# A diffusion block on one core: the second MLP matrix gets a VectorE and ScalarE order written by hand

## The chip, the cores and the metric

The kernel runs on one core of a Trainium2 chip. The metric is the device time of one execution in microseconds (us); the median of three runs before the change is 1617.91 us. A core has a matrix engine (TensorE, "PE" in the profile; its weight loads are "PEld"), an engine for elementwise work on two operands (VectorE, "DVE"), one for functions and casts of one operand (ScalarE, "ACT"), GpSimd ("POOL") and SyncE ("SP"). Here the last two only issue transfers (DMAs) between the device's main memory and the on-chip memory; each has a queue of its own. TensorE accumulates in PSUM, which has eight banks per partition.

## The reference

One layer over 512 tokens of width 2048. The second half of the layer is the MLP, whose second matrix is where the change lies:

```python
def sqrelu_mlp(h, w1, w2):
    return jnp.square(jax.nn.relu(h @ w1)) @ w2
...
x = x + g1 * rms_norm(y_lat, norm_g[i, 1])
x = x + g2 * rms_norm(sqrelu_mlp(modulate(rms_norm(x, norm_g[i, 2]), sh2, sc2), w_mlp_in[i], w_mlp_out[i]), norm_g[i, 3])
```

The hidden width is 8192, so `w2` is 8192 x 2048 in 32-bit floats. Ahead of the MLP come the adaLN vectors, a Fourier mixer and its output matrix.

## The kernel before

**Arithmetic.** Every 32-bit product is made of three faster ones. `split` (L117 to L120) casts an operand on ScalarE to a rounded `hi` and subtracts on VectorE to get the rest, `lo`. `mm3` (L122 to L125) then issues hi x lo, lo x hi and hi x hi into one PSUM bank. TensorE's first matmul of a piece of weights reads its `lo`. There are three `hi` and three `lo` buffers for weights (`NB["hi"]`, L32), in pool `sp`.

**First MLP matrix.** The hidden columns are worked in units of 256. Units 6 to 30 use a form with seven block products in place of eight (Winograd's variant of Strassen's algorithm): `unit(u)` (L779) makes A11, S1, S3, S2, A12, A22, S4, some of them from sums of weight blocks. Unit 31, the last, is done plainly by `unit_plain` (L827). The squared ReLU of each unit goes to device memory `gd` on GpSimd's queue (L647).

**Second MLP matrix.** Rows 0 to 7167 of `w2` are cut into seven chunks (`c`) of 1024 and the output columns into two halves (`j`). For each of the 14 pairs the same seven products are made, 98 in all, each with four pieces of left operand, two halves of weights of 128 x 1024, and 24 matmuls of 512 columns into two banks. The left operands of a chunk are made once by `left_in(c, s)` (L882): A11, A12 and A22 are a cast (L902) and a `lo` (L903) of a quarter of the loaded chunk; S1, S3, S2 and S4 first take a VectorE difference or sum (L891, L894, L897, L900). `g_chunk` (L876) loads a chunk. `second(c, j)` (L907) loads four weight blocks in two halves each and makes the weight sums on VectorE: for S1 (L941), S3 (L946), S2 (L950) and A22 (L954). After the splits of a product, the copies of the product before from PSUM (L928) are issued by `settle`, and one DMA on GpSimd's queue adds the tile to device memory (L930; L932 for the first chunk). `THEN` hangs further work on a product: the next chunk's load, its left operands, and in the last chunk `early`, the load and split of two units for the last part.

The rest of `w2` (hidden rows 7168 to 8191) is done plainly behind that, and the seven partial sums are gathered.

**What sets the order.** The program is traced once. A planner then orders the instructions of each engine and each transfer queue by priority (earlier traced first, `high_priority` moves a part ahead) and by when its own timeline holds them to be ready; the hardware's queues keep that order. Inside `tc.manual_schedule(engines=...)` the named engines keep the traced order among the block's instructions; the kernel uses it once before, at L582, and instructions from outside the block may stand between. `tc.issue_after(x)` queues the work of a block behind `x`. A tile of a pool waits until the slot's last reader is done. The pools of the second matrix (`ga`, `sb`, `s1`, `g4`, L860) lie in the memory of the first part's pool, so a chunk's first loads wait for the products that read there: the first two `ga` tiles lie where the left operands of S2 and S4 were.

The call sequence around the change:

```python
    with tc.high_priority(offset=AHEAD):
        g_chunk(0)
        for s in PRODUCTS:
            cast = left_in(0, s)
...
    for c in range(CHUNKS):
        for j in range(2):
            second(c, j)
    settle()
```

Of the kernel before, what the change touches and what calls it, by code (L numbers as in the profile page):

```python
# [12 lines left out]
ALU = mybir.AluOpType  # L13

P = 128
# [43 lines left out]
def block_kernel(ctx: ExitStack, tc, xs, c_l, w_mod, b_col, g_col,  # L59
# [21 lines left out]
    def hi4(shape):  # L81
        return sp.tile(shape, F32R, tag="hi4", bufs=NB["hi"], name=nm("hi"))
# [22 lines left out]
    def bank(shape=(P, 512)):  # L105
        return psp.tile(list(shape), F32, tag="ps", bufs=8 - NB["mv"], name=nm("ps"))
# [529 lines left out]
    def stream(src):  # L636
        flip[0] ^= 1
        t = raw("raw" if flip[0] else "rawm")
        nc.sync.dma_start(out=t, in_=src)
        return t  # L640
# [138 lines left out]
    def unit(u):  # L779

        b11, b12, b22, b21 = (stream(w_in_s[u - UNIT0, b].rearrange("p k f -> p (k f)")) for b in range(4))

        x_, y_ = bank(), bank()
        a_, b_, c_, d_ = x_[:, T0], x_[:, T1], y_[:, T0], y_[:, T1]

        def product(s, src, ps, start):
            wh, wl = hi4([P, 1024]), lo4([P, 1024])
            split(wh, wl, src)
            for k in range(8):
                ks = slice(k * P, (k + 1) * P)  # L790
                lh, ll = left_of(s, k)
                nc.tensor.matmul(ps, lhsT=wh[:, ks], rhs=ll, start=start and k == 0, stop=False, skip_group_check=True)  # L792
                nc.tensor.matmul(ps, lhsT=wl[:, ks], rhs=lh, start=False, stop=False, skip_group_check=True)  # L793
                nc.tensor.matmul(ps, lhsT=wh[:, ks], rhs=lh, start=False, stop=k == 7, skip_group_check=True)  # L794

        product("A11", b11, a_, True)
        flip[0] ^= 1
        both = raw("raw" if flip[0] else "rawm")
        nc.vector.tensor_add(out=both, in0=b11, in1=b12)
        product("S1", both, d_, True)  # L800
        settle()
        sn, r = tmp4([P, 4, 256]), tmp4([P, 1024])
        nc.scalar.copy(out=sn[:, 0], in_=a_)
        nc.vector.tensor_add(out=b12, in0=b12, in1=b22)
        product("S3", b12, c_, False)
        nc.scalar.copy(out=sn[:, 2:4].rearrange("p a t -> p (a t)"), in_=y_)
        nc.vector.tensor_add(out=b11, in0=b12, in1=b11)
        product("S2", b11, b_, False)
        product("A12", b21, a_, False)
        nc.vector.tensor_add(out=b12, in0=b11, in1=b21)  # L810
        product("A22", b12, c_, False)
        nc.vector.tensor_sub(out=sn[:, 1], in0=sn[:, 0], in1=b_)
        nc.vector.tensor_add(out=sn[:, 2], in0=sn[:, 2], in1=sn[:, 3])
        nc.vector.tensor_add(out=r[:, 768:1024], in0=sn[:, 1], in1=sn[:, 2])
        product("S4", b22, d_, False)
        nc.scalar.activation(out=r[:, 0:256], in_=a_, func=AF.Relu)
        nc.scalar.activation(out=r[:, 768:1024], in_=r[:, 768:1024], func=AF.Relu, scale=-1.0)

        def rest():
            nc.vector.tensor_add(out=r[:, 256:768].rearrange("p (a t) -> p a t", a=2), in0=y_.rearrange("p (a t) -> p a t", a=2),  # L820
                                 in1=sn[:, 1].unsqueeze(1).to_broadcast([P, 2, 256]))
            nc.scalar.activation(out=r[:, 256:512], in_=r[:, 256:512], func=AF.Relu)
            nc.scalar.activation(out=r[:, 512:768], in_=r[:, 512:768], func=AF.Relu, scale=-1.0)
            square_out(u, r.rearrange("p (f t) -> p f t", f=2))
        owed.append(rest)
# [44 lines left out]
    PRODUCTS = ("A11", "S1", "S3", "S2", "A12", "A22", "S4")  # L870
    pacc = {(s, j): dp.tile([P, 2, 512], F32, name=f"p{s}{j}") for s in PRODUCTS for j in range(2)}
    left = [{} for _ in range(CHUNKS)]
    first_cast = []
    raws = [{} for _ in range(CHUNKS + 1)]

    def g_chunk(c):  # L876
        gf = [buf("ga", [P, 4, 512]) for _ in range(2)]
        for j in range(2):
            nc.sync.dma_start(out=gf[j].rearrange("p u t -> p (u t)"), in_=gd[c][:, j].rearrange("p u t -> p (u t)"))
        raws[c]["g"] = gf  # L880

    def left_in(c, s):  # L882

        st = raws[c]
        gf = st["g"]
        a11, a21, a12, a22 = gf[0][:, :, T0], gf[0][:, :, T1], gf[1][:, :, T0], gf[1][:, :, T1]
        if s in ("A11", "A12", "A22"):
            src = {"A11": a11, "A12": a12, "A22": a22}[s]
        elif s == "S1":
            src = st["v"] = tmp4([P, 4, 256])  # L890
            nc.vector.tensor_sub(out=src, in0=a22, in1=a21)  # L891
        elif s == "S3":
            src = tmp4([P, 4, 256])
            nc.vector.tensor_sub(out=src, in0=a11, in1=a21)  # L894
        elif s == "S2":
            src = st["v"]
            nc.vector.tensor_add(out=src, in0=src, in1=a11)  # L897
        else:
            src = st["v"]
            nc.vector.tensor_sub(out=src, in0=src, in1=a12)  # L900
        t = buf("ga" if s == "A11" else "s1" if s == "S1" and c % 2 == 0 else "sb", [P, 2, 4, 256], F32R)
        cast = nc.scalar.copy(out=t[:, 0], in_=src)  # L902
        nc.vector.tensor_tensor(out=t[:, 1], in0=src, in1=as32(t[:, 0]), op=ALU.subtract)  # L903
        left[c][s] = t
        return cast

    def second(c, j):  # L907

        def load(b):
            return [stream(w_out_s[c, j, b, h].rearrange("p k n -> p (k n)")) for h in range(2)]  # L910

        def product(s, src):
            ps = [bank(), bank()]
            for h in range(2):
                wh, wl = hi4([P, 1024]), lo4([P, 1024])
                split(wh, wl, src[h])
                for k in range(2):
                    ks = slice(k * 512, (k + 1) * 512)
                    for i in range(2):
                        ts = slice(i * P, (i + 1) * P)  # L920
                        t = left[c][s]
                        mm3(ps[i], t[:, 0, 2 * h + k, ts], t[:, 1, 2 * h + k, ts], wh[:, ks], wl[:, ks], h + k == 0, h + k == 2)
            settle()

            def out():
                ev = g4([P, 2, 512])
                for i in range(2):
                    nc.scalar.copy(out=ev[:, i, :], in_=ps[i])  # L928
                if c:
                    nc.gpsimd.dma_start(out=pacc[s, j], in_=ev, accum_op=ALU.add)  # L930
                else:
                    nc.gpsimd.dma_start(out=pacc[s, j], in_=ev)  # L932
            owed.append(out)
            for f in THEN.get((c, j, s), ()):
                f()

        b11, b12 = load(0), load(1)
        product("A11", b11)
        both = [g4([P, 1024]) for _ in range(2)]
        for h in range(2):  # L940
            nc.vector.tensor_add(out=both[h], in0=b11[h], in1=b12[h])  # L941
        b22 = load(2)
        with tc.issue_after(first_cast[0]) if c + j == 0 else nullcontext():
            product("S1", both)
        for h in range(2):
            nc.vector.tensor_add(out=b12[h], in0=b12[h], in1=b22[h])  # L946
        product("S3", b12)
        b21 = load(3)
        for h in range(2):
            nc.vector.tensor_add(out=b11[h], in0=b12[h], in1=b11[h])  # L950
        product("S2", b11)
        product("A12", b21)
        for h in range(2):
            nc.vector.tensor_add(out=b12[h], in0=b11[h], in1=b21[h])  # L954
        product("A22", b12)
        product("S4", b22)

    oacc = []

# [19 lines left out]
            nc.vector.scalar_tensor_tensor(out=oacc[2 + i][:, right_c], in0=u2[:, h], scalar=-1.0, in1=p["S1"][:, h], op0=ALU.mult, op1=ALU.subtract)  # L979


    NEXT = {(0, "A12"): ("A11",), (0, "S4"): ("S1",), (1, "A11"): ("S3",), (1, "A12"): ("S2",), (1, "S4"): ("A12", "A22")}
    THEN = {}
    for c in range(CHUNKS - 1):
        THEN[c, 0, "S3"] = [lambda c=c: g_chunk(c + 1)]
        for (j, s), what in NEXT.items():
            THEN[c, j, s] = [lambda c=c, n=n: left_in(c + 1, n) for n in what]
        THEN[c + 1, 0, "S1"] = [lambda c=c: left_in(c + 1, "S4")]

    gts = {}  # L990

# [10 lines left out]
            g_in(u, lambda: (t[:, 0], t[:, 1]))  # L1002
        oacc.extend(buf("sb" if i else "ga", [P, D]) for i in range(4))

    THEN[CHUNKS - 1, 0, "A12"] = [early]
    with tc.high_priority(offset=AHEAD):
        g_chunk(0)
        for s in PRODUCTS:
            cast = left_in(0, s)
            if s == "S1":  # L1010
                first_cast.append(cast.ins)
            if s == "S3":
                with tc.issue_after(cast.ins):
                    act_relu2(UNITS - 1, last)
    for c in range(CHUNKS):
        for j in range(2):
            second(c, j)
    settle()

    f0, f1 = LAST[0]  # L1020
    for n in (0, 2, 1, 3):
# [150 lines left out]
```

## Time and profile before

| | us |
|---|---|
| median of 3 runs (lowest, highest) | 1617.91 (1617.63, 1619.02) |
| the profiled execution | 1621.48 |
| its span, first to last instruction | 1619.7 |
| mean granted TensorE clock in it | 0.991 |
| TensorE busy | 1566.8 |
| VectorE busy | 1251.4 |
| ScalarE busy | 853.6 |
| second matrix in it, from the first matmul of A11 on | from about 965 to 1500 |

The profile shows one execution. An engine's timeline has the start, the duration, the engine, the line, the operation, what it writes and reads, the shapes, and in brackets how long the engine idled before it and whose work ended that idle time; rows of the same kind in a row are merged, with a count (x2). TensorE's durations are modelled, so a step from one start to the next says more than a duration. A line of a helper (L119, L120, L123 to L125) stands for every caller.

### The profile page before, as it was taken

How to read it: one execution, taken by the hardware profiler on the slowest of the kernel's cores; microseconds unless marked ns; L12 is line 12 of the kernel's file. 1: busy time of each engine (PE TensorE's matmuls, PEld its weight loads, DVE VectorE, ACT ScalarE, POOL GpSimd, SP SyncE). 2: the span in 40 equal slices, each digit the busy share in tenths (PEclk: the TensorE clock that was granted, in tenths of full speed). 3: DMA queues.
4: the chain of work that ended last, by engine and by line, in shares of the span. 5: the costliest groups of instructions: out<-in, count | busy, mean ns of one | idle time of the engine just before them, and what ended most of it. 6: DMA issues, size and time to landing. Idle time of an engine off the chain costs nothing.

```text
span 1619.7 us, 24743 instructions
## 1 busy us (share of the span) xinstructions
PE 1566.8 (97%) x9753; PEld 1329.1 (82%) x9753; DVE 1251.4 (77%) x1545; ACT 853.6 (53%) x1235; POOL 106.2 (7%) x144
## 2 busy tenths in 40 slices
PE   5999998999999999999999989999999999999997
PEld 4766664678899999999999977878878787878886
DVE  7776868675888888888777659979797969767687
ACT  7443336335554545455555537757575757665442
POOL 0000000000000000000000000111111111111100
PEclk9999998999999999999999999999999999999999
DMA  9987889886255555555443456779898988888972
GB/s 380 335 294 291 327 321 358 313 310 250 98 179 187 171 172 177 188 179 185 138 130 135 143 183 245 248 199 252 199 249 215 238 219 198 203 212 199 313 280 104
DMA packets 98325, 365.09 MB, mean 225 GB/s; under 512 B 11109, under 2 KB 11125, under 8 KB 95393
## 3 DMA queue, kind: packets, MB, share of 16 engines
q1 hardware_dynamic: 78992, 294.30, 50.7%
q0 software_dynamic: 19216, 69.22, 19.8%
q8 instruction: 76, 1.25, 0.3%
q14 instruction: 41, 0.33, 0.1%
HBM read 286.92 MB, written 76.55 MB: 224 GB/s over the span
## 4 chain that ended last, share of the span: by engine, by line
PE 79%; DVE 10%; DMA 6%; issue 3%; ACT 2%; DVEq 0%; SPq 0%; ACTq 0%
PE ps L123 16%; PE ps L124 16%; PE ps L125 16%; PE ps L793 9%; PE ps L794 8%; PE ps L792 8%; PE mv L206 3%; DMA raw<-in_w_mod 3%; DVE lo L120 2%; PE mv L172 1%; DVE sb L903 1%; DVE raw L946 1%; DMA ga<-gd 1%; DMA raw<-gd 1%; ACT hi L119 1%
## 5 line engine op out<-in xcount | busy, mean ns | idle before, releaser
L120 DVE TENSOR_TENSOR lo<-raw,hi 128x1024 fp32r<-128x1024 f32 x379 | 461.0, 1222 | 185.8 <-ACT hi L119 183.6
L119 ACT CAST hi<-raw 128x1024 fp32r<-128x1024 f32 x379 | 398.3, 1051 | 316.3 <-PE ps L125 147.1
L123 PE MATMUL ps<-lo,sb 128*128 128x512 f32 x608 | 238.0, 391 | 5.7 <-DVE lo L120 5.6
L124 PE MATMUL ps<-hi,sb 128*128 128x512 f32 x608 | 236.6, 389 | 0.0
L125 PE MATMUL ps<-hi,sb 128*128 128x512 f32 x608 | 236.6, 389 | 0.0
L793 PE MATMUL ps<-big,lo 128*128 128x256 f32 x600 | 170.2, 284 | 0.0
L794 PE MATMUL ps<-big,hi 128*128 128x256 f32 x600 | 169.8, 283 | 0.0
L792 PE MATMUL ps<-big,hi 128*128 128x256 f32 x600 | 169.6, 283 | 0.0
L928 ACT COPY g<-ps 128x512 f32<-128x512 f32 x196 | 114.6, 588 | 91.9 <-PE ps L125 83.8
L123 PEld LDWEIGHTS ps<-lo,sb 128*128 128x128 f32 x608 | 114.1, 188 | 34.0 <-DVE lo L120 10.8
L125 PEld LDWEIGHTS ps<-hi,sb 128*128 128x128 f32 x608 | 114.1, 188 | 23.9
L124 PEld LDWEIGHTS ps<-hi,sb 128*128 128x128 f32 x608 | 114.1, 188 | 23.4
L793 PEld LDWEIGHTS ps<-big,lo 128*128 128x128 f32 x600 | 115.2, 192 | 0.3 <-DVE lo L120 0.2
L794 PEld LDWEIGHTS ps<-big,hi 128*128 128x128 f32 x600 | 115.2, 192 | 0.0
L792 PEld LDWEIGHTS ps<-big,hi 128*128 128x128 f32 x600 | 115.1, 192 | 0.0
L793 PE MATMUL ps<-g,lo 128*128 128x256 f32 x400 | 113.8, 285 | 1.1 <-DVE lo L120 1.0
L792 PE MATMUL ps<-s,hi 128*128 128x256 f32 x400 | 113.2, 283 | 0.0
L794 PE MATMUL ps<-s,hi 128*128 128x256 f32 x400 | 113.2, 283 | 0.0
L793 PE MATMUL ps<-s,lo 128*128 128x256 f32 x400 | 113.2, 283 | 0.0
L794 PE MATMUL ps<-g,hi 128*128 128x256 f32 x400 | 113.0, 283 | 0.0
L792 PE MATMUL ps<-g,hi 128*128 128x256 f32 x400 | 112.3, 283 | 0.0
L221 DVE SCALAR_TENSOR_TENSOR row<-raw,sil,row 128x512 f32<-128x512 f32 x105 | 78.2, 749 | 21.8 <-DMA raw<-in_w_mod 20.8
(291 smaller groups left out, 3279.6 us busy)
## 6 DMA issues: line engine op xcount, KB each, us to landing
raw<-in_w_mod SPq DMA_DIRECT2D x192, 512.0 KB, 5.4
raw<-in_w_out_s SPq DMA_DIRECT2D x112, 512.0 KB, 5.7
raw<-in_w_in_s SPq DMA_DIRECT2D x100, 512.0 KB, 3.9
pS<-g POOLq DMA_DIRECT2D x56, 512.0 KB, 6.3
pA<-g POOLq DMA_DIRECT2D x42, 512.0 KB, 7.0
raw<-in_wf SPq DMA_DIRECT2D x32, 512.0 KB, 5.5
gd<-tmp POOLq DMA_DIRECT2D x32, 512.0 KB, 3.8
ga<-gd SPq DMA_DIRECT2D x14, 1024.0 KB, 6.6
```

The costliest lines, as they stand in the source:

```text
L119: nc.scalar.copy(out=hi, in_=src)
L120: return nc.vector.tensor_tensor(out=lo, in0=src, in1=as32(hi), op=ALU.subtract)
L123: nc.tensor.matmul(ps, lhsT=ah, rhs=bl, start=start, stop=False)
L124: nc.tensor.matmul(ps, lhsT=al, rhs=bh, start=False, stop=False)
L125: nc.tensor.matmul(ps, lhsT=ah, rhs=bh, start=False, stop=stop)
L172: nc.tensor.matmul(mv[:, 256 + cb:257 + cb], lhsT=rows[:, cb * P:(cb + 1) * P], rhs=ones[:, 0:1], start=True, stop=True)
L206: nc.tensor.matmul(st["ps"][32 * j:32 * j + 32, 0:256], lhsT=cst[:, kq * 4 + j, :], rhs=t[:, j * 256:(j + 1) * 256], start=(kq == 0), stop ...
L221: nc.vector.scalar_tensor_tensor(out=rows, in0=t[:, j * 512:(j + 1) * 512], scalar=sil[:, kt:kt + 1], in1=rows, op0=ALU.mult, op1=ALU.add)
L792: nc.tensor.matmul(ps, lhsT=wh[:, ks], rhs=ll, start=start and k == 0, stop=False, skip_group_check=True)
L793: nc.tensor.matmul(ps, lhsT=wl[:, ks], rhs=lh, start=False, stop=False, skip_group_check=True)
L794: nc.tensor.matmul(ps, lhsT=wh[:, ks], rhs=lh, start=False, stop=k == 7, skip_group_check=True)
L928: nc.scalar.copy(out=ev[:, i, :], in_=ps[i])
```

## The change

The body of `second` is taken apart into `load`, `fetch`, `product` and `leave_second`, numbered through all 98 products. All VectorE and ScalarE instructions of the second matrix (but for the first two left operands) stand in a `manual_schedule` block, in the order: the two splits of product n, the copies from PSUM of product n - 2, what `THEN` hangs on n, and then `fetch(n)`, the loads and weight sums of product n + 2. The left operands of chunk 0 after the first two move from a high-priority part into `THEN`, as does the ReLU of the last unit. The chunk-0 load goes to GpSimd's queue. In unit 30 the product S4 is made before A12.

```diff
@@ in unit(u)
         product("S2", b11, b_, False)
+        if u == UNITS - 2:
+            product("S4", b22, d_, False)
         product("A12", b21, a_, False)
...
-        product("S4", b22, d_, False)
+        if u < UNITS - 2:
+            product("S4", b22, d_, False)
@@ in g_chunk(c)
-            nc.sync.dma_start(out=gf[j].rearrange("p u t -> p (u t)"), in_=gd[c][:, j].rearrange("p u t -> p (u t)"))
+            queue = nc.sync if c else nc.gpsimd
+            queue.dma_start(out=gf[j].rearrange("p u t -> p (u t)"), in_=gd[c][:, j].rearrange("p u t -> p (u t)"))
@@ in place of second(c, j)
+    SECOND = [(c, j, s) for c in range(CHUNKS) for j in range(2) for s in PRODUCTS]
...
+    def load(c, j, *of):
+        for b in of:
+            blocks[c, j, b] = [stream(w_out_s[c, j, b, h].rearrange("p k n -> p (k n)")) for h in range(2)]
+
+    def fetch(n):
+
+        if n + 2 >= len(SECOND):
+            return
+        c, j, s = SECOND[n + 2]
+        b = [blocks.get((c, j, i)) for i in range(4)]
+        add = nc.vector.tensor_add
+        if s == "A11":
+            load(c, j, 0, 1)
+        elif s == "S1":
+            load(c, j, 2)
+            both = sums[c, j] = [g4([P, 1024]) for _ in range(2)]
+            for h in range(2):
+                add(out=both[h], in0=b[0][h], in1=b[1][h])
+        elif s == "S3":
+            for h in range(2):
+                add(out=b[1][h], in0=b[1][h], in1=b[2][h])
+        elif s == "S2":
+            load(c, j, 3)
+            for h in range(2):
+                add(out=b[0][h], in0=b[1][h], in1=b[0][h])
+        elif s == "A22":
+            for h in range(2):
+                add(out=b[1][h], in0=b[0][h], in1=b[3][h])
+
+    def leave_second(n):
+        c, j, s = SECOND[n]
+        ev = g4([P, 2, 512])
+        for i in range(2):
+            nc.scalar.copy(out=ev[:, i, :], in_=held[n][i])
+        if c:
+            nc.gpsimd.dma_start(out=pacc[s, j], in_=ev, accum_op=ALU.add)
+        else:
+            nc.gpsimd.dma_start(out=pacc[s, j], in_=ev)
+
+    def product(n):
+
+        c, j, s = SECOND[n]
+        src = sums[c, j] if s == "S1" else blocks[c, j, {"A11": 0, "S3": 1, "S2": 0, "A12": 3, "A22": 1, "S4": 2}[s]]
+        ps = held[n] = [bank(), bank()]
+        t = left[c][s]
+        for h in range(2):
+            wh, wl = hi4([P, 1024]), lo4([P, 1024])
+            split(wh, wl, src[h])
...
+        if n > 1:
+            leave_second(n - 2)
+        for f in THEN.get((c, j, s), ()):
+            f()
+        fetch(n)
@@ what hangs on which product
-    NEXT = {(0, "A12"): ("A11",), (0, "S4"): ("S1",), (1, "A11"): ("S3",), (1, "A12"): ("S2",), (1, "S4"): ("A12", "A22")}
+    REST = {(1, "S2"): ("S3",), (1, "A22"): ("S2",), (1, "S4"): ("A12", "A22")}
+    NEXT = ({(0, "S4"): ("A11",), (1, "A11"): ("S1",), **REST}, {(0, "A12"): ("A11",), (0, "S4"): ("S1",), **REST})
...
+    for s, what in (("S1", ("S3",)), ("S3", ("S2",)), ("S2", ("A12", "A22")), ("A12", ("S4",))):
+        for w in what:
+            then(0, 0, s, lambda w=w: left_in(0, w))
     for c in range(CHUNKS - 1):
-        THEN[c, 0, "S3"] = [lambda c=c: g_chunk(c + 1)]
...
+        then(c, 0, "S3" if c else "A22", lambda c=c: g_chunk(c + 1))
+        for (j, s), what in NEXT[min(c, 1)].items():
+            for w in what:
+                then(c, j, s, lambda c=c, w=w: left_in(c + 1, w))
+        then(c + 1, 0, "S1", lambda c=c: left_in(c + 1, "S4"))
...
-    THEN[CHUNKS - 1, 0, "A12"] = [early]
+    then(CHUNKS - 1, 0, "A12", early)
+    then(0, 0, "A11", lambda: act_relu2(UNITS - 1, last))
     with tc.high_priority(offset=AHEAD):
         g_chunk(0)
-        for s in PRODUCTS:
...
+        for s in ("A11", "S1"):
+            left_in(0, s)
+    fetch(-2)
+    with tc.manual_schedule(engines={mybir.EngineType.DVE, mybir.EngineType.Activation}):
+        fetch(-1)
+        for n in range(len(SECOND)):
+            product(n)
+        for n in (2, 1):
+            leave_second(len(SECOND) - n)
```

## Rows read from the trace of the kernel before

**Rows 1.** The page: busy us of each engine, share of span, instructions.
```profile
PE 1566.8 (97%) x9753; PEld 1329.1 (82%) x9753; DVE 1251.4 (77%) x1545; ACT 853.6 (53%) x1235; POOL 106.2 (7%) x144
```

**Rows 2.** Waits of PE, 900 to 1540 us: total us, times, longest.
```profile
PE ps L123 <- DVE lo L120: 11.2, 9, 3.0
PE ps L124 <- DVE ga L903: 4.5, 1, 4.5
```

**Rows 3.** Timeline of PE at three places; start us, us, engine, line.
```profile
969.78 0.80 PE L124 MATMUL ps<-hi,ga 128*128 128x512 f32 x1 [4.46 <-DVE ga L903]
...
1133.36 0.39 PE L125 MATMUL ps<-hi,ga 128*128 128x512 f32 x1
1134.84 0.50 PE L123 MATMUL ps<-lo,s 128*128 128x512 f32 x1 [1.09 <-DVE lo L120]
1135.17 0.40 PE L124 MATMUL ps<-hi,s 128*128 128x512 f32 x1
...
1445.61 0.50 PE L123 MATMUL ps<-lo,ga 128*128 128x512 f32 x1 [3.05 <-DVE lo L120]
```

**Rows 4.** Windows: busy us of each engine (instructions), PE clock, DMA share, GB/s.
```profile
960.00:1000.00 40.00, 33.26 (x139) 26.49 (x138) 39.45 (x35) 26.84 (x33) 2.84 (x5) 0.96 0.43 148
...
1440.00:1480.00 40.00, 36.61 (x155) 29.42 (x154) 27.30 (x24) 22.98 (x29) 5.93 (x7) 0.96 0.86 209
```

**Rows 5.** Timeline of DVE at the start of chunk 2.
```profile
1126.75 1.22 DVE L120 TENSOR_TENSOR lo<-raw,hi 128x1024 fp32r<-128x1024 f32 x1
1127.89 2.35 DVE L941 TENSOR_TENSOR g<-raw,raw 128x1024 f32<-128x1024 f32 x2
1130.16 1.22 DVE L946 TENSOR_TENSOR raw<-raw,raw 128x1024 f32<-128x1024 f32 x1
1131.30 1.22 DVE L903 TENSOR_TENSOR sb<-tmp,sb 128x1024 fp32r<-128x1024 f32 x1
1132.43 1.22 DVE L946 TENSOR_TENSOR raw<-raw,raw 128x1024 f32<-128x1024 f32 x1
1133.57 1.22 DVE L120 TENSOR_TENSOR lo<-g,hi 128x1024 fp32r<-128x1024 f32 x1
```

**Rows 6.** Timeline of DVE at three other places.
```profile
256.04 2.74 DVE L599 SCALAR_TENSOR_TENSOR x<-big,ry,x 128x512 f32<-128x512 f32 x4
258.69 0.69 DVE L559 TENSOR_TENSOR big<-big,big 128x512 f32<-128x512 f32 x1
...
961.69 2.35 DVE L941 TENSOR_TENSOR g<-raw,raw 128x1024 f32<-128x1024 f32 x2
...
968.50 1.22 DVE L903 TENSOR_TENSOR ga<-ga,ga 128x1024 fp32r<-128x1024 f32 x1
...
1023.42 1.22 DVE L891 TENSOR_TENSOR tmp<-ga,ga 128x1024 f32<-128x1024 f32 x1 [0.53 <-DMA ga<-gd]
```

**Rows 7.** Timeline of ACT at several places.
```profile
1024.67 1.05 ACT L902 CAST s<-tmp 128x1024 fp32r<-128x1024 f32 x1 [0.32 <-DVE tmp L891]
...
1038.80 1.10 ACT L928 COPY g<-ps 128x512 f32<-128x512 f32 x2
...
1129.78 1.06 ACT L119 CAST hi<-g 128x1024 fp32r<-128x1024 f32 x1
...
1149.02 1.05 ACT L119 CAST hi<-raw 128x1024 fp32r<-128x1024 f32 x1 [1.19 <-PE ps L125]
...
1154.45 1.05 ACT L119 CAST hi<-raw 128x1024 fp32r<-128x1024 f32 x1 [1.19 <-PE ps L125]
...
1442.12 1.05 ACT L119 CAST ga<-raw 128x1024 fp32r<-128x1024 f32 x1 [2.27 <-DMA raw<-gd]
```

**Rows 8.** The chain that ended last, 940 to 985 us: start us, us, what.
```profile
954.34 7.31 DMA ga<-gd
```

**Rows 9.** Waits of the SP queue, 900 to 1500 us: total us, times, longest.
```profile
SPq L879 <- PE ps L125: 56.3, 6, 10.8
```

**Rows 10.** The page's DMA issues: KB each, median us to landing.
```profile
raw<-in_w_out_s SPq DMA_DIRECT2D x112, 512.0 KB, 5.7
```

More of the change, by code (lines that the diff above doesn't have):

```diff
@@ L872, in block_kernel @@
     left = [{} for _ in range(CHUNKS)]
-    first_cast = []
     raws = [{} for _ in range(CHUNKS + 1)]
@@ L901, in left_in @@
         t = buf("ga" if s == "A11" else "s1" if s == "S1" and c % 2 == 0 else "sb", [P, 2, 4, 256], F32R)
-        cast = nc.scalar.copy(out=t[:, 0], in_=src)
+        nc.scalar.copy(out=t[:, 0], in_=src)
         nc.vector.tensor_tensor(out=t[:, 1], in0=src, in1=as32(t[:, 0]), op=ALU.subtract)
         left[c][s] = t
[L905 to L913, printed above, removed]
-            for h in range(2):
[L915 to L926, printed above, removed]
-                for i in range(2):
[L928 to L956, printed above, removed]
@@ new lines, in block_kernel @@
+    SECOND = [(c, j, s) for c in range(CHUNKS) for j in range(2) for s in PRODUCTS]
+    blocks = {}
+    sums = {}
+    held = {}
+    def load(c, j, *of):
[12 more added lines that the diff above has]
+            both = sums[c, j] = [g4([P, 1024]) for _ in range(2)]
+            for h in range(2):
+                add(out=both[h], in0=b[0][h], in1=b[1][h])
[9 more added lines that the diff above has]
+                add(out=b[1][h], in0=b[0][h], in1=b[3][h])
@@ new lines, in leave_second @@
+    def leave_second(n):
[15 more added lines that the diff above has]
+            split(wh, wl, src[h])
+            for k in range(2):
+                ks = slice(k * 512, (k + 1) * 512)
+                for i in range(2):
+                    ts = slice(i * P, (i + 1) * P)
+                    mm3(ps[i], t[:, 0, 2 * h + k, ts], t[:, 1, 2 * h + k, ts], wh[:, ks], wl[:, ks], h + k == 0, h + k == 2)
+        if n > 1:
[3 more added lines that the diff above has]
+        fetch(n)
@@ L979, in gather, with then @@
             nc.vector.scalar_tensor_tensor(out=oacc[2 + i][:, right_c], in0=u2[:, h], scalar=-1.0, in1=p["S1"][:, h], op0=ALU.mult, op1=ALU.subtract)
-    NEXT = {(0, "A12"): ("A11",), (0, "S4"): ("S1",), (1, "A11"): ("S3",), (1, "A12"): ("S2",), (1, "S4"): ("A12", "A22")}
+    REST = {(1, "S2"): ("S3",), (1, "A22"): ("S2",), (1, "S4"): ("A12", "A22")}
+    NEXT = ({(0, "S4"): ("A11",), (1, "A11"): ("S1",), **REST}, {(0, "A12"): ("A11",), (0, "S4"): ("S1",), **REST})
     THEN = {}
-    for c in range(CHUNKS - 1):
-        THEN[c, 0, "S3"] = [lambda c=c: g_chunk(c + 1)]
-        for (j, s), what in NEXT.items():
-            THEN[c, j, s] = [lambda c=c, n=n: left_in(c + 1, n) for n in what]
-        THEN[c + 1, 0, "S1"] = [lambda c=c: left_in(c + 1, "S4")]
+    def then(c, j, s, f):
+        THEN.setdefault((c, j, s), []).append(f)
+    for s, what in (("S1", ("S3",)), ("S3", ("S2",)), ("S2", ("A12", "A22")), ("A12", ("S4",))):
+        for w in what:
+            then(0, 0, s, lambda w=w: left_in(0, w))
+    for c in range(CHUNKS - 1):
+        then(c, 0, "S3" if c else "A22", lambda c=c: g_chunk(c + 1))
[3 more added lines that the diff above has]
+        then(c + 1, 0, "S1", lambda c=c: left_in(c + 1, "S4"))
     gts = {}
@@ L1003, in early @@
         oacc.extend(buf("sb" if i else "ga", [P, D]) for i in range(4))
-    THEN[CHUNKS - 1, 0, "A12"] = [early]
+    then(CHUNKS - 1, 0, "A12", early)
+    then(0, 0, "A11", lambda: act_relu2(UNITS - 1, last))
     with tc.high_priority(offset=AHEAD):
         g_chunk(0)
-        for s in PRODUCTS:
[L1009 to L1018, printed above, removed]
+        for s in ("A11", "S1"):
[7 more added lines that the diff above has]
+            leave_second(len(SECOND) - n)
     f0, f1 = LAST[0]
```

## The prediction

> **What bounds the kernel now.** I read the busy shares first, then TensorE's waits in the second MLP matrix, then the timelines round those waits. The reader is to see in the busy shares that TensorE (PE) is the bound, at 97% of the span, with VectorE (DVE) at 77% and ScalarE (ACT) at 53% [rows 1]. A change of order can therefore give back only what PE idles in this stretch. The waits say how much that is: between 900 and 1540 us nine waits on the `lo` that VectorE makes, 11.2 us, and one on the left operand of A11 (L903), 4.5 us [rows 2]. A wait costs more than its gap. Where the gap is 1.09 us the matmul starts 1.48 us after the one before it, against 0.23 in the run of matmuls, and the next one 0.33 after that [rows 3]: 1.25 + 0.10, so 0.26 beyond the gap, 2.6 us for ten. The granted clock is 0.96 in the two 40 us windows with the long waits [rows 4], where matmuls go at the lower level after an idle PE: 0.04 x 40 = 1.6 us each, 3.2. Together 15.7 + 2.6 + 3.2 = 21.5 us is all that the stretch can give.
>
> Their causes differ. At each of five chunk starts (1134.84 is one) VectorE does five operations back to back between two `lo`, and the second `lo` is late [rows 5]; price 1.35 each. At the beginning (969.78) it did six weight sums, from 961.69 on, ahead of A11's left `lo` at 968.50 [rows 6]. At 1445.61 [rows 3] a cast waited 2.27 us for a transfer of the last units, ahead of the next weight cast [rows 7].
>
> **The change, what it takes away.** Within the block, VectorE and ScalarE get the traced order. That such a block keeps it is seen in the earlier one: the multiply of L559 runs exactly behind four L599 as traced, at 258.69 [rows 6]. A11's and S1's left operands are now traced before the block and their loads go through GpSimd's queue. Before, those loads land at 954.34 + 7.31 = 961.65 on the chain [rows 8], held behind weight loads in SyncE's queue; the last unit's moved S4 frees their memory two products earlier. VectorE is no longer busy with the six sums, so A11 starts on time. The early casts now come behind A12 of the last chunk, four products after that chunk's start, and their transfer is there by then. The five chunk-start bursts also go, since sums are issued a product earlier. So all 21.5 us go, with what comes next priced below. Moving S4 adds no instruction, and PE has no such wait in unit 30; nothing is charged. The later copies from PSUM free a pair of banks after two products instead of one; three pairs rotate and the copies (1.10 us for two [rows 7]) run beside matmuls: nothing. The chunk loads of c = 0 on GpSimd's queue stand before that queue's write of the last units, which is read only at the end: nothing.
>
> **What it adds.** The number of operations is the same, but the queue now waits in its order. Per product VectorE has two `lo`, then the left pieces that are hung on that product, then the two sums for the product after next. Prices: two sums are 2.27 us from start to start (1127.89, x2, to 1130.16 [rows 5]), so 1.135 for one operation. A left operand made by a difference is subtract, cast on ScalarE, `lo`. From the subtract at 1023.42 to its cast at 1024.67 is 1.25 [rows 6, 7], the cast takes 1.05 and 0.03 to the next start, the `lo` 1.135: 3.47. In the traced order nothing else stands between subtract and `lo`, so VectorE idles 1.2 us of it, time in which the planner before was free to put other work. Subtract, `lo` and two sums together are 5.74 us between two `lo` that PE needs.
>
> How much is free? A product lasts 5.43 us (casts at 1149.02 and 1154.45 [rows 7]). Only three `hi` and three `lo` buffers exist, so no `lo` can be earlier than about one half-product ahead, and the chunk-start burst shows the limit: five operations, 5.68 us, between the `lo` of 1126.75 and that of 1133.57, make PE 1.25 us late [rows 3, 5]. So about 4.4 us are free, and 5.74 makes it 1.33 late, 1.44 with the restart. The cover is gone, and `lo` is what is late next.
>
> Now count, with j the column half. In a full chunk (c = 1 to 5) these products carry too much: (0, S1): left S4 and sums, 5.74. (0, S4): left S1 and sums, 5.74. (1, S2): left S3 and sums, 5.74. (1, S4): the two left casts of A12 and A22, which stand behind two copies on ScalarE, their `lo`, and sums, about 5.4, late by 1.0. All others stay at 3.5 or less. After (1, S4) comes A11 with sums, so VectorE is still 0.2 behind at the next (0, S1), which becomes 1.55 late. Chunk 0 carries more: left S3 in (0, S1), S2 in (0, S3), A12 and A22 in (0, S2), S4 in (0, A12), S1 in (1, A11). Chunk 6 has left S4 alone.
>
> Sum: 12 bursts of 5.74 by themselves ((0, S4) five times, (1, S2) six, (0, S1) of chunk 0) x 1.44 = 17.3. (1, S4) six times x 1.11 = 6.7. (0, S1) of chunks 1 to 6 x 1.66 = 10.0. Chunk 0 otherwise: (0, S2) with the debt of (0, S3), 1.8; (1, A11) behind a loaded (0, S4), 2.5; two small ones, 0.6. In all 38.9 us in 28 waits. Idle times of this length (1.09 gap) show no slower matmuls behind them [rows 3], so no clock is charged.
>
> Net +38.9 - 21.5 = +17.4 us. The profiled execution is 1621.5 (span 1619.7 and 1.8 around it), so 1638.9 there; it is 3.6 above the median of the runs, 1617.9, so the median becomes about **1635 us**.
>
> Bounds of a burst, which no row shows in this form: if the cast were wholly covered, 4.54 us, 0.15 late, 0.25 with restart; 26 bursts 6.5, and the change gains 15 (1603). If each burst also caught 0.4 us of late transfers or copies, 10 more: 1645. I take 1.35 to 1.66, as the nearest row is a burst of almost the same length with its measured lateness.
>
> One rule of the Trainium skill speaks against the part on the chunk starts. The row shows a 1.09 us gap before the same product in five chunks, ended by `lo`, with the `hi` cast done at 1129.78 + 1.06 and VectorE busy throughout [rows 3, 5, 7]. "Perfetto Trace Analysis", section "Optimization Strategy", says that a gap that repeats can mean too little SBUF for the next tile, so that order would not cure it. This case's trace does not agree for these five: VectorE's queue, not a buffer, was late. By the rule the five gaps stay.
>
> **Rivals.** (a) The cast is covered and the bursts cost little: 1603. For it: ScalarE is 53% busy and could be early. Against it: the cast needs the subtract just before it in VectorE's own queue. This is the case on the other side; it decides from a burst of 0.83 us or less (21.5 / 26), that is one of some 5.2 us. (b) The gaps at chunk starts come from buffers, stay at 5 x 1.35 = 6.8, and the new order adds nothing: 1617.9 - 14.7 = 1603. Against it: the rows just named. (c) The two effects cancel, bursts at about 0.8: 1617. (d) The fixed order makes VectorE wait for weights: SyncE's queue stood up to 10.8 us for a buffer of the chunk load [rows 9], a weight tile lands in 5.7 [rows 10], against two products, 10.9, that the earlier sums leave. Late by 5.6 in six chunks, 34 us: 1669. Against it: the buffers of the next chunk's load are now free in the traced order before it is issued. (e) The block is not strictly kept and the change only repairs the two ends, about 14 us: 1604. Against it: the order at 258.69.
>
> **How the numbers follow.** Forecast 0.60, (a) 0.16, (b) 0.04, (c) 0.07, (d) 0.09, (e) 0.04. Faster by over 0.2% is (a), (b), (e): 0.24; within 0.2% (3.2 us, about what a measurement of this kernel can tell from no change) is (c): 0.07; slower 0.69. The likeliest case alone is 1627 to 1644. The range of 1602 to 1646 reaches down to half of the faster cases and leaves out (d).
>
> **What would show it.** Right: A11 of chunk 0 starts without the 4.46 us wait; no wait at 1445; some 28 waits on `lo`, before the S3 and the second half's A11 and A12 of each chunk and before its first A11, each with a VectorE row of L891 to L903 in front that idled for a cast. Wrong: fewer than ten waits, or waits ended by transfers. The prediction falls if VectorE shows other work between the subtract and its `lo`.

## The result and the profile after

| | before | after |
|---|---|---|
| median us (lowest, highest; runs) | 1617.77 (1614.90, 1619.02; 4) | 1635.82 (1632.28, 1636.98; 4) |
| ratio after / before, 95% interval | | 1.011 [1.009, 1.0131] |
| profiled execution, its span | 1621.48, 1619.7 | 1632.28, 1630.5 |

The change made the kernel 18 us slower; 1635 was forecast. The two profiled executions lie only 10.8 us apart, because the one of before lies above all runs of its kernel in this table and the one of after is the fastest of its own. Ahead of the second matrix, where the program hardly differs, the one of after is 4.8 us earlier (first matmul of A11 at 959.87 against 964.70). From that matmul to the last one of the execution it takes 660.4 us against 644.4: 16.0 us more, and this is the stretch to explain.

The page of the kernel after, busy us and share of the span, beside [rows 1]:

```profile
PE 1562.7 (96%) x9753; PEld 1322.6 (81%) x9753; DVE 1253.4 (77%) x1545; ACT 841.8 (52%) x1235; POOL 107.3 (7%) x146
```

The work is the same to a few us on each engine. What differs is who waits. First the waits of PE from 900 to 1560 us in the kernel after (total us, times, longest), which answer to [rows 2]:

```profile
PE ps L123 <- DVE lo L120: 30.6, 26, 2.1
```

Ten waits with 15.7 us have become 26 with 30.6, all on the weights' `lo`. PE's timeline of the kernel after shows the first matmuls of A11 (`ga` is its left operand), and then one wait of each of the three kinds with a gap over 1 us, all in the first full chunk:

```profile
959.87 0.61 PE L123 MATMUL ps<-lo,ga 128*128 128x512 f32 x2
960.41 0.50 PE L124 MATMUL ps<-hi,ga 128*128 128x512 f32 x1
...
1058.29 0.50 PE L123 MATMUL ps<-lo,sb 128*128 128x512 f32 x1 [1.34 <-DVE lo L120]
...
1086.96 0.50 PE L123 MATMUL ps<-lo,ga 128*128 128x512 f32 x1 [1.13 <-DVE lo L120]
1087.29 0.39 PE L124 MATMUL ps<-hi,ga 128*128 128x512 f32 x1
...
1110.16 0.50 PE L123 MATMUL ps<-lo,sb 128*128 128x512 f32 x1 [1.13 <-DVE lo L120]
```

The reader is to see that A11 now follows the last unit without a pause, where [rows 3] had 4.46 us, and that S3 (1058.29), the second half's A11 (1086.96) and its A12 (1110.16) wait, which they did not before. (S3 of chunk 0 is the one place that waited in both: 1.65 us before, 2.04 after.) The step after a gap of 1.13 is again 0.33. The windows of the kernel after, in the columns of [rows 4], stand at the full clock:

```profile
960.00:1000.00 40.00, 36.50 (x157) 28.63 (x156) 32.57 (x29) 25.85 (x32) 3.36 (x6) 1.00 0.52 186
1440.00:1480.00 40.00, 37.91 (x166) 30.69 (x165) 32.44 (x29) 26.27 (x34) 5.94 (x7) 1.00 0.80 203
```

Why `lo` is late is in VectorE's waits of the kernel after, 955 to 1500 us, and in its timeline ahead of 1086.96. L905 and L906 are now the cast and the `lo` of a left operand, L894 a left difference, L931 and L934 weight sums:

```profile
DVE lo L120 <- ACT hi L119: 81.4, 58, 4.2
DVE sb L906 <- ACT sb L905: 29.7, 31, 1.1
DVE ga L906 <- ACT ga L905: 4.1, 6, 0.7
DVE s L906 <- ACT s L905: 3.3, 3, 1.1
```

```profile
1078.79 1.23 DVE L120 TENSOR_TENSOR lo<-raw,hi 128x1024 fp32r<-128x1024 f32 x1 [1.49 <-ACT hi L119]
1079.93 1.22 DVE L894 TENSOR_TENSOR tmp<-ga,ga 128x1024 f32<-128x1024 f32 x1
1082.27 1.23 DVE L906 TENSOR_TENSOR s<-tmp,s 128x1024 fp32r<-128x1024 f32 x1 [1.12 <-ACT s L905]
1083.41 2.35 DVE L931 TENSOR_TENSOR g<-raw,raw 128x1024 f32<-128x1024 f32 x2
1085.68 2.35 DVE L120 TENSOR_TENSOR lo<-raw,hi 128x1024 fp32r<-128x1024 f32 x2
```

The longest group, 81.4 us on the weights' `hi`, is not the cause. ScalarE's own longest wait in that stretch is before these very casts, for TensorE, and no wait of PE above is ended by a cast:

```profile
ACT hi L119 <- PE ps L125: 154.1, 94, 4.4
```

The rows at 1079.93 to 1085.68 are the burst of the prediction: subtract, 1.12 us of idling for ScalarE's cast, `lo` of the left operand, two sums, and only then the weights' `lo`. From 1079.93 to 1085.68 it is 5.75 us, where 5.74 was worked out. The two sums behind the idle time were ready (in lo_behind_sums, below, they run in just that place), and in the fixed order VectorE doesn't take them first. The Trainium skill, "Perfetto Trace Analysis", section "Per-instruction lifecycle: what the profiler-reported window actually captures", calls VectorE and ScalarE strictly first in, first out; these rows agree.

### The profile page after: what moved, and what is told of

The parts are those of the page before. It is cut to its first block, busy times and chain, and to the rows that moved or that the text cites. A ratio compares the mean times of both kernels' runs of the same rounds, so it can differ in the third digit from the quotient of the medians.

```text
span 1630.5 us, 24549 instructions
## 1 busy us (share of the span) xinstructions
PE 1562.7 (96%) x9753; PEld 1322.6 (81%) x9753; DVE 1253.4 (77%) x1545; ACT 841.8 (52%) x1235; POOL 107.3 (7%) x146
## 3 DMA queue, kind: packets, MB, share of 16 engines
q8 instruction: 76, 1.25, 0.3%
## 4 chain that ended last, share of the span: by engine, by line
PE 60%; issue 24%; DVE 7%; DMA 4%; POOL 3%; ACT 1%; SPq 0%; POOLq 0%; DVEq 0%; ACTq 0%
PE ps L793 10%; PE ps L792 10%; PE ps L794 10%; PE ps L123 9%; PE ps L124 8%; PE ps L125 8%; PE mv L206 3%; DVE lo L120 2%; POOL pS L949 2%; DMA raw<-in_w_out 1%; DMA raw<-in_w_mod 1%; POOL pA L949 1%; DMA pS<-g 1%; PE mv L172 1%; DMA x<-in_xs 1%
## 5 line engine op out<-in xcount | busy, mean ns | idle before, releaser
L947 ACT COPY g<-ps 128x512 f32<-128x512 f32 x196 | 104.5, 583 | 1.2 <-PE ps L125 1.0
```

Source lines behind the costliest of these rows:

```text
L947: nc.scalar.copy(out=ev[:, i, :], in_=held[n][i])
```

## The experiments

Each was timed beside runs of the kernel before on the same chip. These had medians of 1619.39 us for the first four kernels and 1617.99 for the other four. Short diffs are against the kernel after.

| kernel | median us | ratio to before, 95% | PE's waits 900 to 1560: us, times |
|---|---|---|---|
| after | 1635.82 | 1.011 [1.009, 1.0131] | 30.6, 26 |
| lo_behind_sums | 1607.89 | 0.9934 [0.9919, 0.9949] | 5.4, 16 |
| spread | 1601.10 | 0.9892 [0.9877, 0.9907] | 4.4, 3 |
| planner_order | 1615.42 | 0.9975 [0.9965, 0.9985] | 13.8, 12 |
| start_undone | 1634.96 | 1.0102 [1.0087, 1.0117] | 29.9, 26 |
| spread_all | 1597.44 | 0.9873 [0.9858, 0.9889] | 1.5, 2 |
| sum_twice | 1646.55 | 1.017 [1.0155, 1.0186] | 35.5, 26 |
| spread_copies_early | 1608.33 | 0.9940 [0.9924, 0.9957] | 11.2, 11 |
| spread_sums_near | 1612.03 | 0.9962 [0.9946, 0.9979] | 11.9, 7 |

Every kernel has one wait of 0.5 to 1.0 us some way behind the second matrix. In the last column it is counted for all but after, start_undone and sum_twice, where it comes after 1560 us.

**lo_behind_sums.** The same order, but the `lo` of each left operand is issued behind the product's sums. No operation is added or taken away.

```diff
         nc.scalar.copy(out=t[:, 0], in_=src)
-        nc.vector.tensor_tensor(out=t[:, 1], in0=src, in1=as32(t[:, 0]), op=ALU.subtract)
+        low = lambda: nc.vector.tensor_tensor(out=t[:, 1], in0=src, in1=as32(t[:, 0]), op=ALU.subtract)
...                                   # in product(n)
         fetch(n)
+        for f in behind:
+            f()
```

> The changed kernel with one thing moved: in a left operand the `lo` is issued behind the two weight sums of the same product, so the sums stand between subtract and `lo` and cover the cast. Theory 1 (VectorE stands still for the cast in the middle of a burst): a burst shrinks from 5.74 to 4.54 us, its lateness from 1.25 to about 0.1 or 0.2; about 9 us of TensorE waits are left, most of them in chunk 0, and the time falls by some 25 to 1605 to 1612. Theory 2 (the sums a product earlier and the copies a product later cost, by weights or buffers that come late): both are as they were, so it stays at 1630 to 1637. Theory 3 (any fixed order costs, whatever it is): 1630 to 1637 too.

The waits of PE in this kernel:

```profile
PE ps L123 <- DVE lo L120: 5.4, 16, 1.1
```

and VectorE's timeline at the burst that was shown for the kernel after (L937 and L909 are the sums and the left `lo` here):

```profile
1077.72 2.35 DVE L937 TENSOR_TENSOR g<-raw,raw 128x1024 f32<-128x1024 f32 x2
1079.99 1.22 DVE L909 TENSOR_TENSOR s<-tmp,s 128x1024 fp32r<-128x1024 f32 x1
```

The gaps before S3 shrink from 1.34 to about 0.18 us, those of the first A11 from 0.74 to 0.23, and the two of 1.13 go (chunks 1 to 6). The sums now fill the time of the cast, and the left `lo` starts without a wait. By the ratios (1.011 - 0.9934, of 1618) this is worth 28 us, more than the whole loss. It is the nearest test of the prediction's central step, and it held.

**spread.** The left operands of chunks 1 to 6 hang on products that carry no sums (S3, A12, A22). The exceptions are pieces without a difference, a cast and a `lo`, which stand beside two sums: A22 on (1, S4), and of chunk 1 also A11 and A12. All keep their `lo` directly behind their cast. From chunk 1 on the load of the next chunk is also issued two products earlier, at (0, A11).

```diff
+            {(0, "A12"): ("A11",), (0, "A22"): ("S1",), (1, "S3"): ("S3",), (1, "A12"): ("S2",), (1, "A22"): ("A12",), (1, "S4"): ("A22",)})
...
-        then(c, 0, "S3" if c else "A22", lambda c=c: g_chunk(c + 1))
+        then(c, 0, "A11" if c else "A22", lambda c=c: g_chunk(c + 1))
...
-        then(c + 1, 0, "S1", lambda c=c: left_in(c + 1, "S4"))
+        then(c + 1, 0, "S3", lambda c=c: left_in(c + 1, "S4"))
+    then(1, 0, "S1", lambda: left_in(1, "A22"))
```

> The changed kernel with the left operands of chunks 1 to 6 hung on products that carry no sums ((0, S3), (0, A22), (1, S3), (1, A12), (1, A22)), subtract, cast and `lo` still together; chunk 0 as it was. No product of chunks 1 to 6 then carries more than 4.4 us. Theory 1: the four waits per chunk go, 5 x 5.6 + 2.7 + some 3 in the second half of chunk 0 = 33 us less: 1600 to 1606, though VectorE idles for the casts as often as before. Theory 1b (it is the idling for casts itself that costs, 37 us in all, wherever it stands): no change, 1630 to 1637. Theory 2 and 3: 1630 to 1637.

PE's waits, VectorE's longest group on left casts, and VectorE's timeline at one such cast in this kernel:

```profile
PE ps L123 <- DVE lo L120: 4.4, 3, 2.0
```

```profile
DVE sb L906 <- ACT sb L905: 33.5, 37, 1.1
```

```profile
1070.92 1.22 DVE L894 TENSOR_TENSOR tmp<-ga,ga 128x1024 f32<-128x1024 f32 x1
1073.25 1.22 DVE L906 TENSOR_TENSOR s<-tmp,s 128x1024 fp32r<-128x1024 f32 x1 [1.12 <-ACT s L905]
1074.40 2.35 DVE L120 TENSOR_TENSOR lo<-raw,hi 128x1024 fp32r<-128x1024 f32 x2
```

VectorE idles for casts as long as in the kernel after (33.5 us against 29.7), and still PE waits in the second matrix only twice, in chunk 0 (2.04 and 1.48 us; the third wait, 0.93 us at 1540.14, lies behind it). Here 1070.92 to 1074.40 is 3.48 us between two `lo`, below the 4.4 that are free. So the idle time alone costs nothing; idle time together with two sums in one product does. The number of buffers is the same as in the kernel after. That speaks against buffers as the cause, the thought behind rival (b), too: the Trainium skill, "Perfetto Trace Analysis", section "Optimization Strategy", reads a gap that repeats as a possible lack of memory for the next tile, and here the repeating gaps of 0.74 to 1.34 us went by order alone, in this run and in lo_behind_sums.

**planner_order.** The kernel after with the fixed order taken off (`manual_schedule` replaced by nothing), all else kept.

> The changed kernel without the fixed order: the same tracing order, sums a product ahead and copies a product later, but the planner orders VectorE and ScalarE as in the kernel before. Theory 1: the planner slips other work into the cast's time; waits of TensorE fall to those of the kernel before or less, 5 to 20 us: 1600 to 1618. Theory 2 (the earlier sums and later copies cost): 1628 to 1637, as they are still there.

PE's waits in this kernel:

```profile
PE ps L123 <- DVE lo L120: 7.6, 10, 2.2
PE ps L124 <- DVE ga L906: 4.1, 1, 4.1
PE ps L123 <- ACT ga L905: 2.1, 1, 2.1
```

It is this fixed order that costs, not the earlier sums or the later copies: without it the kernel is 0.25% below before, and 22 us below after by the ratios (1.011 - 0.9975, of 1618). That any fixed order costs is not so: lo_behind_sums and spread keep one and are faster than this kernel. But the planner brings back the late start of A11 (2.1 and 4.1 us at 967.20 and 972.05), which the fixed order had removed. Round the chunk starts the gaps are 0.4 to 0.6 us, not 1.1, and stand before the second half of the S4 ahead of the chunk, not before its S1. The wait of 3.05 at 1445.61 [rows 3] has become two of 0.24 and 0.39, although ScalarE's timeline here has the casts of `early` at the start of the last chunk, as before, and the first still waits for its transfer:

```profile
1439.51 1.05 ACT L119 CAST ga<-raw 128x1024 fp32r<-128x1024 f32 x1 [3.33 <-DMA raw<-gd]
```

The earlier sums fit this; that they did it isn't shown.

**start_undone.** S4 of unit 30 stands in its old place again, and the chunk-0 load is on SyncE's queue; the fixed order is kept.

> The changed kernel with S4 of unit 30 back at its old place and chunk 0's load back on SyncE's queue; fixed order kept. In the changed kernel's trace that load was issued at 941.96, behind the write of unit 30 on GpSimd's queue, some 4 us after TensorE was done with S4, and the left operand of A11 was ready before TensorE needed it at 959.9. So these two parts should give nothing: within 3 us of the changed kernel, 1632 to 1639, and no wait at the first A11. Rival: they are what repaired the start, and the 4.5 to 6 us wait there comes back: 1639 to 1643.

```profile
PE ps L123 <- DVE lo L120: 29.9, 26, 2.1
```

These are PE's waits in this kernel, 26 as in the kernel after (30.6 us), and A11 starts without a wait here too. These two parts of the change give nothing that can be measured.

**spread_all.** spread, with lo_behind_sums, and in chunk 0 the left operands A22 and S4 one product later each.

> The spread kernel with chunk 0 treated as well: its A22 and S4 operands each hang one product later, so that no product of chunk 0 makes two, and every left `lo` goes behind the sums of its product. The spread kernel has three waits left, 2.04, 1.48 and 0.02 us, all in chunk 0. Theory 1: the first falls to about 0.8 (the subtract still waits for its buffer), the second goes: some 2.5 us less than spread, 1598 to 1600. Rival (the rest of chunk 0 is set by its transfers): no change, 1600 to 1603.

```profile
PE ps L123 <- DVE lo L120: 1.5, 2, 0.8
```

These are PE's waits. One of 0.83 us is left in the second matrix, in chunk 0; the other, 0.71 us at 1536.41, lies behind it, as does the third one of spread, which the expectation took for 0.02 us in chunk 0. The time came out just under what was expected. It is the fastest kernel of the study, 20.5 us below before and, by the ratios, 38 below after. Its interval overlaps that of spread, so that it beats spread isn't shown by the times; the waits (4.4 to 1.5) say it by about the amount that the ratios show (3.1 us).

**sum_twice.** The kernel after with one sum made twice, in the burst of (0, S4) of chunks 1 to 5, and in (0, S2) of chunks 1 to 6, a product without left work.

```diff
+            if j and 0 < c < CHUNKS - 1:
+                add(out=both[0], in0=b[0][0], in1=b[1][0])
...
+            if c and not j:
+                add(out=b[1][0], in0=b[0][0], in1=b[3][0])
```

Both write the same sum a second time, so the result stays the same.

> The changed kernel with one weight sum made twice, to the same result, at eleven places: in chunks 1 to 5 the first sum for S1 of the second half, in the burst of (0, S4), and in chunks 1 to 6 the first sum for A22 of the first half, in (0, S2), which carries two sums and nothing else. Theory 1: the first five cost their whole 1.135 us (the waits before A11 of the second half, 1.13 each, become 2.26) and the six others nothing: 5.7 us more, 1639 to 1643. Rival (VectorE's work as a whole counts): 11 x 1.135 = 12.5 more, 1646 to 1650, with new waits before A12 of the first half.

PE's timeline at the second half's A11 in two chunks, and the windows behind them, in this kernel:

```profile
1090.78 0.58 PE L123 MATMUL ps<-lo,ga 128*128 128x512 f32 x1 [2.27 <-DVE lo L120]
1091.15 0.63 PE L124 MATMUL ps<-hi,ga 128*128 128x512 f32 x1
1091.57 0.63 PE L125 MATMUL ps<-hi,ga 128*128 128x512 f32 x1
...
1259.80 0.50 PE L123 MATMUL ps<-lo,ga 128*128 128x512 f32 x1 [2.27 <-DVE lo L120]
1260.13 0.39 PE L124 MATMUL ps<-hi,ga 128*128 128x512 f32 x1
```

```profile
1090.00:1098.00 8.00, 7.22 (x25) 5.86 (x26) 6.78 (x7) 2.76 (x4) 0.29 (x1) 0.79 0.36 69
1259.00:1267.00 8.00, 7.20 (x32) 5.97 (x33) 8.00 (x8) 3.84 (x5) 0.85 (x1) 1.00 0.45 77
```

All five gaps grow from 1.13 to 2.27, by the 1.14 of one operation, and no new gap comes where the sum was added to a free product: the place decides, as the theory said. But the time came out 4 us above what was expected, and by itself it would fit the rival; it is the gaps that decide. In three of the five chunks the matmuls behind the gap go at the lower clock level for a while (steps of 0.43, granted clock 0.79 over 8 us), in two not (1.00). From that matmul to the next wait it is 24.76 us in the first chunk shown and 23.19 in the second, 1.6 us for each spell, 4.7 for three. 5 x 1.14 + 4.7 = 10.4, and the ratios (1.017 - 1.011, of 1618) say 9.7. How often the clock fell in the other timed runs isn't shown.

**spread_copies_early.** spread with the copies from PSUM back at one product later.

```diff
-        if n > 1:
-            leave_second(n - 2)
+        if n:
+            leave_second(n - 1)
```

> The spread kernel with the copies from PSUM one product later taken back: behind the splits of product n the copies of n - 1, in ScalarE's fixed order. ScalarE then stands until TensorE ends product n - 1, and the next `hi` starts about half a us later than it could; `lo` is still some 2.3 us ahead. Theory 1: no product comes over what is free, so no new wait: within 3 us of spread, 1598 to 1605. Theory 2 (the later copies carry the gain): a wait in most products, 10 us or more, above 1610.

This missed: the time lies above the first range and below the second. PE's waits, VectorE's waits on left casts, and ScalarE's and VectorE's timelines at one of them, all of this kernel (L947 is the copy):

```profile
PE ps L123 <- DVE lo L120: 11.2, 11, 2.0
```

```profile
DVE sb L906 <- ACT sb L905: 48.5, 37, 1.9
...
DVE ga L906 <- ACT ga L905: 11.6, 6, 2.0
```

```profile
1048.65 1.27 ACT L947 COPY g<-ps 128x512 f32<-128x512 f32 x2 [0.98 <-PE ps L125]
1049.81 1.05 ACT L905 CAST sb<-ga 128x1024 fp32r<-128x1024 f32 x1
```

```profile
1050.89 1.23 DVE L906 TENSOR_TENSOR sb<-ga,sb 128x1024 fp32r<-128x1024 f32 x1 [1.76 <-ACT sb L905]
```

The copies wait for PE's last matmul (0.98 us), the left cast stands behind them in ScalarE's order, and VectorE waits for the cast: 60.1 us in these two groups against 37.4 in spread. PE's waits grow by 6.8 us, and the time by 7.8 (0.9940 - 0.9892, of 1618). There are eight new waits of 0.85 us. Each follows one of the few products of spread that still carry a left cast and two sums: six stand before the first A11 of a chunk, behind (1, S4) with A22 or A12, one before the S3 of chunk 1 (the rows shown), and one before the second half's A11 of chunk 0, behind (0, S4) with A11. Where no sums stand in the product, the longer wait for the cast costs nothing. The copies one product later are thus worth some 7 to 8 us here.

**spread_sums_near.** spread with the sums one product ahead, not two, and the left operands hung anew on the products that then carry no sums (S2, A22, S4). Two stay beside sums: A12 and A22 of chunk 1, on its own A11 and S1.

```diff
-        c, j, s = SECOND[n + 2]
+        c, j, s = SECOND[n + 1]
```

> The spread kernel with the sums one product ahead taken back: product n is followed by the sums of product n + 1, and the left operands hang on the products that then carry no sums ((0, S2), (0, A22), (0, S4) and those of the second half). The first `hi` of a product must then wait for a sum that VectorE made just before, some 1.25 us, which still leaves `lo` 2 us ahead. Theory 1 (only the size of what stands between two `lo` matters): few waits outside chunk 0, within 5 us of spread, 1599 to 1607. Theory 2 (the earlier sums carry the gain): waits at every product with sums, 56 in all, of 0.5 us or more: above 1625.

This missed in size. PE's waits, PE's timeline at the longest one and VectorE's in chunk 0, in this kernel:

```profile
PE ps L123 <- DVE lo L120: 11.9, 7, 3.5
```

```profile
1526.48 0.80 PE L123 MATMUL ps<-lo,ga 128*128 128x512 f32 x1 [3.50 <-DVE lo L120]
```

```profile
973.49 1.23 DVE L906 TENSOR_TENSOR sb<-tmp,sb 128x1024 fp32r<-128x1024 f32 x1 [1.11 <-ACT sb L905]
974.63 2.35 DVE L934 TENSOR_TENSOR raw<-raw,raw 128x1024 f32<-128x1024 f32 x2
```

The products with sums don't wait one by one, which a lead worth something by itself would have shown. Three gaps lie in chunk 0 (2.16, 2.44 and 1.26 us), where left operands and sums still meet in a product (973.49 and 974.63). Two more follow products where the same holds: 0.85 us in chunk 1, behind its A22, and 0.90 us in the last chunk, behind `early`. One of 3.50 us comes behind the second matrix, at 1526.48, with matmuls at the lower clock behind it. There, weight casts on ScalarE wait 6.96 and 2.76 us for transfers, and the `lo` (1525.20) stands behind eight operations of the final gathering; which of the two makes it late was not tried. So this run does not give the lead of the sums a price.

## Why the prediction was right, by its steps

**The 26 bursts.** It counted 28 waits and 38.9 us. There are 26; with the gaps as measured and 0.26 for each restart they make 30.6 + 6.8 = 37.4 us.

| place of the wait (the burst before it) | predicted | measured gap + 0.26 |
|---|---|---|
| S3, chunks 1 to 6 ((0, S1)) | 6 x 1.66 | 6 x 1.60 |
| second A11, chunks 1 to 5 ((0, S4)) | 5 x 1.44 | 5 x 1.39 |
| second A12, chunks 0 to 5 ((1, S2)) | 6 x 1.44 | 6 x 1.39 |
| first A11, chunks 1 to 6 ((1, S4)) | 6 x 1.11 | 6 x 1.00 |
| chunk 0, other | 1.44, 1.8, 2.5, 0.6 | 2.30, 1.70, 2.40, none |

The step from the length of a burst to its lateness was the one that had no row of its own; [rows 5] gave it from a burst of almost the same length, and it came out within about 0.1 us for every kind in chunks 1 to 6. In chunk 0 it did not: (0, S1) was put at 1.44 and cost 2.30. Its burst is as long as the others (966.15 to 971.90, 5.75 us), but VectorE comes to it 0.9 us later against what TensorE needs than to the one at 1079.93; just before, it idled 1.25 us at 962.73 for a weight cast that stood behind the last unit's ReLU on ScalarE. The sum took this burst without such a debt. That the ReLU makes it is argued, not tried. lo_behind_sums and spread show the cause from two sides: fill the idle time, or move it to a product without sums, and the waits go.

**What is given back.** The start, the wait at 1445 and the five chunk-start gaps all went, with the clock in both windows; with the three small waits that the sum also counted, 21.5 us. 37.4 - 21.5 = 15.9, and the stretch from A11 on took 16.0 more in the two profiles, where 17.4 was forecast. The forecast 1635 and the median 1635.82 differ by less than the runs do. That they lie within 1 us is luck: the net is the difference of two larger sums, and each spell of the lower clock moves an execution by 1.6 us.

**Where a step was wrong without costing.** The start was put down in part to the load on GpSimd's queue and to the moved S4. start_undone shows that neither matters, and planner_order, which has both, starts late again with all six sums ahead of A11's `lo` at 970.78. VectorE's order repaired the start. It did so with little to spare: of the six sums two still stand ahead of that `lo` in the kernel after, which ends at 960.35, just before the matmul at 960.41 that reads it. VectorE's timeline of the kernel after:

```profile
956.86 2.36 DVE L934 TENSOR_TENSOR raw<-raw,raw 128x1024 f32<-128x1024 f32 x2
959.13 1.22 DVE L906 TENSOR_TENSOR ga<-ga,ga 128x1024 fp32r<-128x1024 f32 x1
```

Nor was A11's load late before. The prediction read the landing at 961.65 on the chain [rows 8] as that of A11's load, but ScalarE's timeline of the kernel before has A11's cast earlier:

```profile
960.42 1.05 ACT L902 CAST ga<-ga 128x1024 fp32r<-128x1024 f32 x1
```

The prediction also had the chunk-0 load standing before GpSimd's write of the last units. GpSimd's timeline of the kernel after shows it behind one such write (the one at 941.39, of unit 30) and ahead of the other (962.06, of unit 31):

```profile
941.39 0.68 POOL L647 DMA_DIRECT2D gd<-tmp  x1 [19.48 <-ACT tmp L646]
941.96 1.21 POOL L882 DMA_DIRECT2D ga<-gd  x2
962.06 0.68 POOL L647 DMA_DIRECT2D gd<-tmp  x1 [18.89 <-ACT tmp L646]
```

and the DMA issues of that kernel from 940 to 960 us (KB each, median us from issue to landing) give their time:

```profile
ga<-gd POOLq DMA_DIRECT2D x2, 1024.0 KB, 11.7
```

The middle of the two landings is about 954, still before A11's first matmul at 959.87.

**Terms that were set at nothing.** The copies one product later were charged nothing. In the order of spread they are worth some 7 to 8 us, through ScalarE's queue. In the kernel after itself that was not tried, so how much of its bursts they already hold down stays open. The clock was charged nothing, by a row with a gap of 1.09 us, although the sum itself had 2.5 us before one product of chunk 0. In the profile of the kernel after that holds: from 960 to 1500 us the granted clock is 1.00. In those of start_undone and sum_twice the clock falls behind both chunk-0 waits of over 2 us. The mean clock of the other timed runs of the kernel after, 0.993 to 0.995 against 0.997 in the profiled one, points the same way: they are 3.1 to 4.7 us longer.

**The rivals.** (a) fell: a cast right behind its subtract is not covered, 1.12 us each. (b) fell with the five gaps at chunk starts, which are not among the 26 of the kernel after, and with the 37.4 us that the new order adds. (c) fell with the size of the bursts. (d) fell: no wait of VectorE on a weight transfer is among its groups after. (e) fell: the timeline has the traced order, and without the block the time is 22 us lower.

## What to carry to other kernels

When an order is written out by hand, find for each engine every place where it hands work to another engine and takes it back, and put that engine's own ready work between the two: here this alone, the same operations in a fixed order, took the time from 1635.8 to 1607.9 us; with the left operands also moved to other products it came to 1597.4. Price a burst by the time between two results that the bounding engine needs (here 4.4 us free in a product of 5.43), not by an engine's share of busy time, which is 77% in the slow kernel and 79% in the fastest. A queue that only drains results, as ScalarE's copies, is worth moving later where a cast that somebody waits for stands behind it, as it did in spread.

## What the runs showed of the hardware

From 900 to 1560 us of the ten profiles, an idle TensorE of up to 1.73 us was never followed by a fall of the clock to its lower level, and with each of the four idles of 3.05 to 4.46 us it fell. Of the 16 idles between 2.04 and 2.44 us eight were followed by one (a seventeenth, 2.12 us in planner_order, runs into one of 4.12 us and is left out). The same gap in the same place went either way: 2.04 and 2.14 us in chunk 0 left the clock at 1.00 in the profile after and at 0.79 over 8 us in that of start_undone. These are counts, not a rule. Each such spell costs 1.6 us in sum_twice. So, as an estimate from that, two executions with equal waits can differ by some 3 us, which is about as much as the profiled execution of after lies below its median.
